# Two heads' attention scores computed together, a maximum moved from DVE to ACT, and fourteen low weight parts made by adding transfers

## The chip, the core and the metric

The kernel runs on one core of one Trainium2 chip. The metric is the device time of one execution in microseconds, smaller being better. Three runs of the kernel before gave 821.81, 825.79 and 827.91 us, so its median is 825.79 us. The core has five engines that work side by side and wait for each other by semaphores: TensorE (PE in the profile, its weight loads apart as PEld), VectorE (DVE), ScalarE (ACT), GpSimd (POOL) and SyncE (SP, which here only issues transfers). Each engine runs its own instructions in a fixed order, so an instruction that waits holds up everything behind it on that engine.

## The reference

One layer with three residual parts: a token mixer (stick-breaking attention with 8 heads of 64, a Conformer convolution branch and a state-space branch), a cross-attention into 256 memory tokens, and a SwiGLU feed-forward part. The sequence is 512 tokens of 1024 channels, all in float32. The change touches the stick-breaking attention and the loads of some weights:

```python
z = jnp.einsum('bhqd,bhkd->bhqk', qb, kh).astype(jnp.float32) * scale
mask = key_pos[None, :] < q_pos[:, None]
log_1mb = jnp.where(mask, jax.nn.log_sigmoid(-z), 0.0)
later = lax.cumsum(log_1mb, axis=3, reverse=True) - log_1mb
w = jnp.where(mask, jnp.exp(jax.nn.log_sigmoid(z) + later), 0.0)
return jnp.einsum('bhqk,bhkd->bhqd', w.astype(vh.dtype), vh)
```

The kernel uses that log_sigmoid(z) + later equals z minus the sum of softplus(z) over this key and all later ones, with softplus(z) = max(z, 0) + ln(1 + exp(-|z|)). So one weight is exp(z - running sum of softplus), the running sum going from the last key backwards.

## The kernel before

All matrix products are made of three products in a reduced float format (`mm3`, lines 114 to 116): each operand is split into a high part (a cast on ACT) and a low part (what is left), and high times high, low times high and high times low are added up in PSUM. Weights come through `load_w` (line 89): SP issues the load of a 128x1024 piece, ACT casts the high part (line 96), and the low part is made in one of two ways. Without `queue`, DVE subtracts the high part from the loaded piece (line 101). With `queue`, ACT writes the negated high part (line 98) and POOL issues a second transfer from memory that adds the weight to it (line 99). `load_k` (line 104) raises the priority of such a load by `EV_QUEUE`, so that it is started earlier. There are three buffers for loaded pieces and four each for high and low parts.

A scheduler orders the instructions of each engine from the program's order, priorities and its own estimates; parts in `tc.manual_schedule` keep the written order on the engines named.

The stage that the change touches is the attention chain `sb_chain` (line 774). It goes over four pairs of heads, and over six groups in each pair (`GROUPS`, line 707): one head with query block 3 (512 keys), block 2 (384 keys), or blocks 1 and 0 together (256 and 128 keys), the two heads of the pair in turn. `sb_weights` (line 709) makes the weights of a group: three products of 64 rows and a masking product into one of two PSUM banks with the tag `z` (lines 721 to 724), then on ACT the absolute value, exp and ln(1 + x) (lines 729 to 731), on DVE the maximum of z and zero added to it (line 732), the running sum (line 734), and z minus that (line 735), and exp on ACT again (line 736). For the groups with two blocks the running sum is one instruction over 384 columns, with a constant tile `seg` of ones and one zero that cuts it between the blocks; else a column of ones stands in its place. Two groups later (`DEPTH` is 2) `sb_turn` (line 743) transposes the weights on PE (line 748) and splits them (lines 120 and 121), and after the last group `sb_out` multiplies them with v.

After each group the chain yields a number (`SB_FILL`, the PE time in ns to be filled), and `weave` lets that much of other PE work in: the projections of the later pairs, the end of the convolution branch, the output projections `mixed_out` (line 804), the memory's norm, the keys of the cross-attention `kv("xa_wk", ...)` (line 862) and the output projection of the attention `out_sb` (line 813). In `mixed_out`, `out_sb` and `kv` the low parts of the weights are made on DVE; only the projections `sb_proj` (line 670), and two pieces in the feed-forward part, use the adding transfer.

Of the kernel before, what the change touches and what calls it, by code (L numbers as in the profile page):

```python
# [11 lines left out]
F32 = mybir.dt.float32  # L12
F32R = mybir.dt.float32r
AF = mybir.ActivationFunctionType
ALU = mybir.AluOpType
# [3 lines left out]
P = 128  # L19
SEQ = 512  # L20
D = 1024
KD = D // P
# [18 lines left out]
TQ, TK, TP = 4, 2, 2  # L41
# [31 lines left out]
def layer(ctx: ExitStack, tc: tile.TileContext, A: dict, out: bass.AP, dbg=None):  # L73
    nc = tc.nc
    v, s, g, te = nc.vector, nc.scalar, nc.gpsimd, nc.tensor
# [3 lines left out]
    const = ctx.enter_context(tc.tile_pool(name="const", bufs=1))  # L79
# [5 lines left out]
    def ps(tag, name):  # L85
        n = {"acc": 4, "z": 2, "tp": 2}[tag]
        return pp.tile([P, 512], F32, tag=tag, bufs=n, name=name)
# [16 lines left out]
    def load_k(w, k, n, name, queue=False):  # L104

        with tc.high_priority(offset=EV_QUEUE if queue else 0):
            return load_w(w[:, k:k + 2, :].rearrange("p k n -> p (k n)"), 2 * n, name, queue)
# [4 lines left out]
    def mm3(o, a, b, start, stop):  # L112

        te.matmul(o, a[0], b[0], start=start, stop=False)  # L114
        te.matmul(o, a[0], b[1], start=False, stop=False)  # L115
        te.matmul(o, a[1], b[0], start=False, stop=stop)  # L116
# [139 lines left out]
    ones1 = const.tile([P, 1], F32, name="ones1")  # L256
# [3 lines left out]
    pk = const.tile([P, NPK], F32, name="pk")  # L260
    negm = const.tile([P, P], F32R, name="negm")
    identr = const.tile([P, P], F32R, name="identr")
    seg = const.tile([P, 384], F32, name="seg")
    gqs = const.tile([P, 1], F32, name="gqs")
    rb = const.tile([P, 3, NT], F32, name="rb")

# [416 lines left out]
    def v_wait():  # L683

        return [x[:, 3, :].rearrange("p (t h d) -> p t h d", t=NT, h=2) for x in mxs]
# [20 lines left out]

    GROUPS = ((0, (3,)), (1, (3,)), (0, (2,)), (1, (2,)), (0, (1, 0)), (1, (1, 0)))

    def sb_weights(p, gi, qkT, sbp):

        qT, kT = qkT
        hh, qbs = GROUPS[gi]
        w = sum(qb + 1 for qb in qbs) * P
        r0 = slice(hh * 64, hh * 64 + 64)
        z = ps("z", f"z{p}{gi}")
        o = 0
        for qb in qbs:
            nk = (qb + 1) * P
            zo = z[:, o:o + nk]
            q, k = [x[r0, qb * P:(qb + 1) * P] for x in qT], [x[r0, 0:nk] for x in kT]  # L720
            te.matmul(zo, q[0], k[0], start=True, stop=False)  # L721
            te.matmul(zo, q[0], k[1], start=False, stop=False)
            te.matmul(zo, q[1], k[0], start=False, stop=False)
            te.matmul(zo[:, qb * P:], identr, negm, start=False, stop=True)  # L724
            o += nk
        ta = sbp.tile([P, SEQ], F32, tag="sba", bufs=2, name=f"sa{p}{gi}")[:, :w]
        ts = sbp.tile([P, SEQ], F32, tag="sbs", bufs=4, name=f"ss{p}{gi}")[:, :w]
        z = z[:, :w]
        s.activation(ta, z, AF.Abs)  # L729
        s.activation(ta, ta, AF.Exp, scale=-1.0)  # L730
        s.activation(ta, ta, AF.Ln, bias=1.0)  # L731
        v.scalar_tensor_tensor(ta, z, 0.0, ta, op0=ALU.max, op1=ALU.add)  # L732
        d0 = ones1.to_broadcast([P, w]) if len(qbs) == 1 else seg[:, ::-1]
        v.tensor_tensor_scan(ts[:, ::-1], d0, ta[:, ::-1], 0.0, op0=ALU.mult, op1=ALU.add)  # L734
        v.tensor_tensor(ts, z, ts, op=ALU.subtract)  # L735
        s.activation(ts, ts, AF.Exp)  # L736
        return ts
# [36 lines left out]
    def sb_chain(sbp):  # L774
        sqa = sbp.tile([P, SEQ], F32, name="sqa")
        wTs, pend = {}, []
        fronts = {0: sb_front(0, pr[0][0], sbp)}
        yield FRONT_FILL

        def turn():  # L780
            p, gi, ts = pend.pop(0)
            if gi == 0:
                wTs[p] = [[sbp.tile([P, 3, SEQ], F32R, tag=f"wT{i}{hh}", name=f"wT{i}{p}{hh}") for hh in range(2)] for i in "hl"]
            sb_turn(p, gi, ts, wTs[p])
            if gi == len(GROUPS) - 1:
                sb_out(p, wTs.pop(p), pr[p][1], sbp, sqa)

        for p in range(NPAIR):
            for gi in range(len(GROUPS)):
                pend.append((p, gi, sb_weights(p, gi, fronts[p], sbp)))  # L790
                if len(pend) > DEPTH:
                    turn()
                yield SB_FILL[p * 6 + gi]
                if gi == FRONT and p + 1 < NPAIR:
                    fronts[p + 1] = sb_front(p + 1, pr[p + 1][0], sbp)
                    if p + 1 == 3:
                        for x, y in zip(pr[3][1], v_wait()):
                            g.tensor_copy(x[:, :, ::2, :], y)
        while pend:
            turn()  # L800
        branch_rstd([sqa], 512, 0, sbp)


    def mixed_out(src, bi, ks, k0, hf):
        c = slice(hf * 512, hf * 512 + 512)
        acc = [ps("acc", f"wo{hf}{bi}{t}") for t in range(NT)]
        yield from gemm_rows(acc, lambda k, t: [x[:, k - k0, t * P:(t + 1) * P] for x in src], A["w_out"][hf], 512, ks,
                             f"wo{hf}{bi}", ks[0], ks[-1])
        for t in range(NT):
            with tc.high_priority(offset=EV_OUT):  # L810
                v.scalar_tensor_tensor(xr[:, t, c], acc[t], rb[:, bi, t:t + 1], xr[:, t, c], op0=ALU.mult, op1=ALU.add)  # L811

    def out_sb(ks):

        if ks[0] == 0:
            xacc.extend(ps("acc", f"wos{t}") for t in range(NT))
        for k in ks:
            if k % 2 == 0:
                wos[k // 2] = load_k(A["w_out"][0], k, 512, f"wos{k}")
            for t in range(NT):  # L820
                mm3(xacc[t], [x[:, k, t * P:(t + 1) * P] for x in mxs], cols(wos[k // 2], slice((k % 2) * 512, (k % 2) * 512 + 512)), k == 0, k == 3)
            tick()
            yield 2600

    xacc, wos = [], {}
# [36 lines left out]
    def kv(nm, hf):  # L862
        acc = [ps("acc", f"{nm}{hf}{t}") for t in range(2)]
        hm = mem["hm"]
        yield from gemm_rows(acc, lambda k, t: [hm[:, i, k, t * P:(t + 1) * P] for i in range(2)], A[nm][hf], 512, range(KD),
                             f"{nm}{hf}", 0, KD - 1, TK)
        for t in range(2):
            if nm == "xa_wv":
                c = slice(hf * 512, hf * 512 + 512)
                split(*[x[:, t, c] for x in mem["v"]], acc[t])  # L870
                continue
            kn = cvp.tile([P, 2, 256], F32, tag=("cpr", "ac")[t], name=f"kn{hf}{t}")
            ss = cvp.tile([P, 2], F32, tag="kss", bufs=2, name=f"kss{hf}{t}")
            av = acc[t].rearrange("p (h d) -> p h d", h=2)
            for h in range(2):
                s.activation(kn[:, h, :], av[:, h, :], AF.Square, accum_out=ss[:, h:h + 1])
            r = rstd(ss, 256, cvp, 2, "kr")
            for h in range(2):
                v.scalar_tensor_tensor(kn[:, h, :], av[:, h, :], r[:, h:h + 1], mem["g"], op0=ALU.mult, op1=ALU.mult)
            late.append([3 + t, lambda t=t, kn=kn: k_turn(hf, t, kn)])  # L880
# [10 lines left out]
    with tc.tile_pool(name="ssmp", bufs=1, side="right") as sp:  # L891
# [80 lines left out]
        with tc.manual_schedule(engines={v.engine, s.engine, g.engine}):  # L972
            for b in range(3):
                for x in vzs[b]:
                    g.memset(x[:, :, 1, :].bitcast(F32), 0.0)
            aside(18)
            squares(0)
            aside(2)
            scale(0)
            squares(1)  # L980
            turn(0)
            aside(2)
            u_high(0)
            scale(1)
            low(0)
            turn(1)
            squares(2)
            aside(99)
            g.memset(hp[:, :, :CPAD], 0.0)
            g.memset(tmpm, -2.0 ** 100)  # L990
            g.affine_select(out=tmpm, in_=tmpm, pattern=[[1, P]], compare_op=ALU.is_ge, fill=0.0, base=0, channel_multiplier=-1)
            g.memset(seg, 1.0)
            g.memset(seg[:, 255:256], 0.0)
            u_low(0)
            low(1)
            u_high(1)
            squares(3)
            scale(2)
            turn(2)
            u_low(1)  # L1000
            scale(3)
            turn(3)
            low(2)
            low(3)
            next(S5)
# [34 lines left out]
    kT = mem["k"]  # L1040
    with tc.tile_pool(name="xa", bufs=1, side="right") as xa:
# [29 lines left out]
        with tc.tile_pool(name="xq", bufs=1, side="right") as xq:  # L1071
            PT = [xq.tile([P, 2, 2, SEQ], F32R, name="PT" + i) for i in "hl"]
            qT = [xq.tile([P, 4, SEQ], F32R, name="qT" + i) for i in "hl"]
# [94 lines left out]
    with tc.tile_pool(name="ff", bufs=1, side="right") as ff:  # L1168
# [239 lines left out]
        for _, t, hf in slots:  # L1408
            for k in range(TAIL):
                step(NF - TAIL + k, *ops[k], t, hf)  # L1410
            c = slice(hf * 512, hf * 512 + 512)
# [59 lines left out]
```

## Time and profile before

| | |
|---|---|
| median of three runs | 825.79 us |
| profiled execution | 827.81 us, of which the span between its first and last instruction is 826.1 us |
| ACT busy over the span | 408.8 us (49%) |
| POOL busy over the span | 181.9 us (22%) |
| chain of work that ended last | PE 80%, DVE 12%, ACT 3% of the span |
| attention scores, first and last product (line 721) | 141.5 us and 283.8 us |

A profile gives for each engine the time that it was busy. A busy PE is not PE at its peak: its matrix products overlap, and its clock can be granted at half. The granted clock stands beside each stretch, 1.00 being full. The waits view says for which instruction an engine stood idle. In the lines of a group, the number behind x is how many there were, then come the busy time in us, the mean of one in ns, and the idle time before them.

### The profile page before, as it was taken

The page shows a single profiled execution, that of the slowest core. Times are in us where ns is not written, and L with a number is a line of the kernel's source. Part 1 is how long each engine was busy: PE and PEld are TensorE (multiplying, and loading weights), DVE is VectorE, ACT ScalarE, POOL GpSimd, SP SyncE. Part 2 cuts the span into 40 slices and gives each one's busy share as a digit, 9 for nine tenths or more (in the row PEclk, how much of TensorE's full clock was granted, in tenths as well). Part 3 has the DMA queues.
Part 4 walks back from the last instruction along what each step waited for, and adds up shares of the span by engine and source line. Part 5 has one row for each costly group of instructions (what it writes and reads, how often), then busy time and mean ns, then how long its engine had stood idle before and what let it go on. Part 6 is the DMA issues. An engine that isn't in the chain of part 4 may idle for free.

```text
span 826.1 us, 12223 instructions
## 1 busy us (share of the span) xinstructions
PE 786.6 (95%) x4640; PEld 689.5 (83%) x4640; DVE 632.4 (77%) x1095; ACT 408.8 (49%) x747; POOL 181.9 (22%) x157
## 2 busy tenths in 40 slices
PE   5699999999989999999999789999999999999998
PEld 3678999887767878888888689999999999888886
DVE  8979989789897968566856688899899998333333
ACT  6344375987667836354634653444444443323321
POOL 4910021001000000000000006577666671000000
PEclk9979999999888999999999979999999999999999
DMA  6233588543013423420442323333333321222322
GB/s 219 71 84 61 112 171 166 116 144 117 33 45 109 119 87 100 130 77 27 125 138 69 77 77 102 104 102 102 104 103 107 127 100 57 97 98 81 102 77 102
DMA packets 25115, 83.41 MB, mean 101 GB/s; under 512 B 3041, under 2 KB 3297, under 8 KB 25058
## 3 DMA queue, kind: packets, MB, share of 16 engines
q1 hardware_dynamic: 22466, 75.31, 28.7%
q0 software_dynamic: 2592, 7.34, 5.9%
q8 instruction: 36, 0.59, 0.3%
q14 instruction: 21, 0.17, 0.1%
HBM read 80.54 MB, written 2.10 MB: 100 GB/s over the span
## 4 chain that ended last, share of the span: by engine, by line
PE 80%; DVE 12%; ACT 3%; issue 2%; DMA 1%; POOL 0%; POOLq 0%; DVEq 0%
PE fo L114 5%; PE fo L116 5%; PE fo L115 5%; PE f L116 2%; PE f L115 2%; PE f L114 2%; PE xo L114 2%; PE xo L115 2%; PE qkv L114 2%; PE xo L116 2%; PE qkv L116 2%; PE qkv L115 2%; PE xq L114 2%; PE xq L115 2%; PE xq L116 2%
## 5 line engine op out<-in xcount | busy, mean ns | idle before, releaser
L618 DVE SCALAR_TENSOR_TENSOR cac<-hp,pk,cac 128x512 f32<-128x512 f32 x60 | 42.4, 748 | 0.0
L1251 POOL TENSOR_TENSOR wgb<-wgb 128x512 f32<-128x512 f32 x18 | 31.8, 1769 | 40.2 <-DMA wgb<-in_w_gu_dram 33.2
L1276 POOL TENSOR_TENSOR wga<-wga 128x512 f32<-128x512 f32 x20 | 28.8, 1439 | 43.5 <-DVE wga L1275 43.5
L1271 POOL DMA_DIRECT2D wa00lo<-in_w_gu_dram x1 | 0.9, 877 | 159.9 <-ACT wa00lo L1270 159.9
L1324 POOL TENSOR_TENSOR aF<-aF,fup 128x1024 f32<-128x1024 f32 x10 | 34.2, 3424 | 6.0 <-DVE fup L1320 5.1
L1252 POOL TENSOR_TENSOR wgb<-wga,wgb 128x512 f32<-128x512 f32 x18 | 35.4, 1965 | 0.3
L772 POOL TENSOR_TENSOR sqa<-sqa,sq 128x512 f32<-128x512 f32 x3 | 4.0, 1332 | 92.7 <-ACT sq L771 59.3
L1275 DVE TENSOR_TENSOR wga<-wgb,wga 128x512 f32<-128x512 f32 x22 | 22.9, 1039 | 0.0
L121 DVE TENSOR_TENSOR wTl<-wT,wTh 128x384 fp32r<-128x384 f32 (+2 forms) x40 | 16.3, 415 | 2.1 <-ACT wTh L120 2.0
L729 ACT ACTIVATE sa<-z 128x384 f32<-128x384 f32 (+1 forms) x24 | 12.6, 524 | 10.3 <-PE z L724 10.0
L120 ACT CAST wTh<-wT 128x384 fp32r<-128x384 f32 (+2 forms) x40 | 14.5, 369 | 6.2 <-PE wT L748 4.9
L734 DVE TENSOR_TENSOR_SCAN ss<-ones,sa 128x512 f32<-128x512 f32 (+1 forms) x16 | 17.3, 1082 | 0.0
L721 PE MATMUL z<-kh,qh 64*128 64x512 f32 (+3 forms) x32 | 13.6, 426 | 3.2 <-DVE ss L735 3.1
L736 ACT ACTIVATE ss<-ss 128x384 f32<-128x384 f32 (+1 forms) x24 | 13.5, 561 | 6.0 <-DVE ss L735 5.5
L732 DVE SCALAR_TENSOR_TENSOR sa<-z,sa 128x384 f32<-128x384 f32 (+1 forms) x24 | 14.2, 594 | 2.8 <-ACT sa L731 2.8
L721 PEld LDWEIGHTS z<-kh,qh 64*128 64x128 f32 x32 | 6.2, 192 | 10.8 <-DVE ss L735 5.2
L811 DVE SCALAR_TENSOR_TENSOR xr<-wo,rb,xr 128x512 f32<-128x512 f32 x16 | 11.9, 744 | 3.5 <-PE wo L116 3.2
L735 DVE TENSOR_TENSOR ss<-z,ss 128x384 f32<-128x384 f32 (+1 forms) x24 | 14.2, 592 | 0.0
L730 ACT ACTIVATE sa<-sa 128x384 f32<-128x384 f32 (+1 forms) x24 | 13.6, 565 | 0.3
L731 ACT ACTIVATE sa<-sa 128x384 f32<-128x384 f32 (+1 forms) x24 | 13.5, 564 | 0.3
L1322 ACT ACTIVATE aF<-aF 128x1024 f32<-128x1024 f32 x11 | 11.6, 1057 | 4.0 <-DVE aF L1320 2.9
L748 PE MATMUL wT<-ident,ss 128*128 128x128 f32 x80 | 12.6, 276 | 0.0
(2210 smaller groups left out, 3276.3 us busy)
## 6 DMA issues: line engine op xcount, KB each, us to landing
wgb<-in_w_gu_dram SPq DMA_DIRECT2D x22, 512.0 KB, 3.2
wga<-in_w_gu_dram SPq DMA_DIRECT2D x22, 512.0 KB, 3.4
for<-in_w_fo_dram SPq DMA_DIRECT2D x22, 512.0 KB, 3.3
xr<-in_x_dram SPq DMA_DIRECT2D x4, 512.0 KB, 5.1
out_dram<-xr SPq DMA_DIRECT2D x8, 256.0 KB, 2.0
xbh<-in_x_dram SPq DMA_DIRECT2D x2, 512.0 KB, 4.7
xbl<-in_x_dram SPq DMA_DIRECT2D x2, 512.0 KB, 7.6
mt<-in_mem_dram SPq DMA_DIRECT2D x2, 512.0 KB, 4.0
```

Source lines behind the costliest of these rows:

```text
L114: te.matmul(o, a[0], b[0], start=start, stop=False)
L115: te.matmul(o, a[0], b[1], start=False, stop=False)
L116: te.matmul(o, a[1], b[0], start=False, stop=stop)
L121: v.tensor_tensor(lo, src, hi, op=ALU.subtract)
L618: v.scalar_tensor_tensor(a, x, w, a, op0=ALU.mult, op1=ALU.add)
L721: te.matmul(zo, q[0], k[0], start=True, stop=False)
L734: v.tensor_tensor_scan(ts[:, ::-1], d0, ta[:, ::-1], 0.0, op0=ALU.mult, op1=ALU.add)
L1251: eng.tensor_tensor(b[:, 0], b[:, 1], b[:, 2], op=ALU.add)
L1252: eng.tensor_tensor(b[:, 1], a[:, 0], b[:, 1], op=ALU.subtract)
L1275: v.tensor_tensor(a[:, 0], b[:, 0], a[:, 0], op=ALU.subtract)
L1276: eng.tensor_tensor(a[:, 1], a[:, 1], a[:, 0], op=ALU.subtract)
L1324: (g if i + 1 < len(units) else v).tensor_tensor(aF[p], aF[p], dst, op=ALU.mult)
```

## The change

The products of the scores leave `sb_weights` and become `sb_scores`, which writes those of both heads of a pair, alternating, into both `z` banks before either head's further steps. On ACT, `sb_weights` gets one more instruction, the maximum of z and zero (Relu) into the tile of the running sum; the DVE instruction that did this is gone. The running sum takes two tensors, adding both; it is one instruction for each query block, and `seg` with its two memsets on POOL is gone. The loads in `mixed_out`, `out_sb` and `kv` for `xa_wk` use the adding transfer: 4 + 2 + 8 = 14 loads.

```diff
-    def sb_weights(p, gi, qkT, sbp):
+    def sb_scores(p, gi, qkT):
         qT, kT = qkT
-        hh, qbs = GROUPS[gi]
+        qbs = GROUPS[gi][1]
+        zs = [ps("z", f"z{p}{gi + hh}") for hh in range(2)]
+        with tc.manual_schedule(engines={te.engine}):
+            o = 0
+            for qb in qbs:
+                nk = (qb + 1) * P
+                for n, (i, j) in enumerate(((0, 0), (0, 1), (1, 0))):
+                    for hh, z in enumerate(zs):
+                        r0 = slice(hh * 64, hh * 64 + 64)
+                        te.matmul(z[:, o:o + nk], qT[i][r0, qb * P:(qb + 1) * P], kT[j][r0, 0:nk], start=n == 0, stop=False)
+                for z in zs:
+                    te.matmul(z[:, o + qb * P:o + nk], identr, negm, start=False, stop=True)
+                o += nk
+        return zs
+
+    def sb_weights(p, gi, z, sbp):
...
         s.activation(ta, z, AF.Abs)
+        s.activation(ts, z, AF.Relu)
         s.activation(ta, ta, AF.Exp, scale=-1.0)
         s.activation(ta, ta, AF.Ln, bias=1.0)
-        v.scalar_tensor_tensor(ta, z, 0.0, ta, op0=ALU.max, op1=ALU.add)
-        d0 = ones1.to_broadcast([P, w]) if len(qbs) == 1 else seg[:, ::-1]
-        v.tensor_tensor_scan(ts[:, ::-1], d0, ta[:, ::-1], 0.0, op0=ALU.mult, op1=ALU.add)
+        o = 0
+        for qb in qbs:
+            c = slice(o, o + (qb + 1) * P)
+            v.tensor_tensor_scan(ts[:, c][:, ::-1], ta[:, c][:, ::-1], ts[:, c][:, ::-1], 0.0, op0=ALU.add, op1=ALU.add)
+            o += (qb + 1) * P
         v.tensor_tensor(ts, z, ts, op=ALU.subtract)
         s.activation(ts, ts, AF.Exp)
         return ts
...
             for gi in range(len(GROUPS)):
-                pend.append((p, gi, sb_weights(p, gi, fronts[p], sbp)))
+                if gi % 2 == 0:
+                    zs = sb_scores(p, gi, fronts[p])
+                pend.append((p, gi, sb_weights(p, gi, zs[gi % 2], sbp)))
...
         yield from gemm_rows(acc, lambda k, t: [x[:, k - k0, t * P:(t + 1) * P] for x in src], A["w_out"][hf], 512, ks,
-                             f"wo{hf}{bi}", ks[0], ks[-1])
+                             f"wo{hf}{bi}", ks[0], ks[-1], queue=True)
...
-                wos[k // 2] = load_k(A["w_out"][0], k, 512, f"wos{k}")
+                wos[k // 2] = load_k(A["w_out"][0], k, 512, f"wos{k}", True)
...
         yield from gemm_rows(acc, lambda k, t: [hm[:, i, k, t * P:(t + 1) * P] for i in range(2)], A[nm][hf], 512, range(KD),
-                             f"{nm}{hf}", 0, KD - 1, TK)
+                             f"{nm}{hf}", 0, KD - 1, TK, queue=nm == "xa_wk")
```

## What was predicted

> **What bounds the kernel now.** I read the page first, then the busy times of stretches around the attention stage, then what PE waited for there, then the groups of instructions by line and shape, last the order in time.
>
> ```profile
> span 826.1 us, 12223 instructions
> PE 786.6 (95%) x4640; PEld 689.5 (83%) x4640; DVE 632.4 (77%) x1095; ACT 408.8 (49%) x747; POOL 181.9 (22%) x157
> ```
>
> Over the whole span PE is the busy engine. The change works between about 141 us, where the first score product starts, and 289 us, where the last weights of the chain are made. In that stretch the shares differ (columns: stretch and its length, then busy us and instructions of each engine, granted clock of PE, share of the DMA engines, GB/s):
>
> ```profile
> 141.00:289.00 148.00, 141.55 (x692) 111.89 (x691) 129.39 (x252) 112.53 (x256) 6.71 (x6) 0.93 0.35 98
> 207.20:214.00 6.80, 6.80 (x24) 5.42 (x22) 4.54 (x14) 4.28 (x11) 0.00 (x0) 0.51 0.22 81
> 231.10:234.50 3.40, 3.40 (x13) 2.95 (x13) 3.40 (x7) 3.11 (x6) 0.00 (x0) 0.52 0.00 0
> 244.80:255.00 10.20, 9.87 (x29) 7.69 (x30) 6.91 (x14) 4.63 (x8) 0.00 (x0) 0.51 0.44 125
> 260.00:280.00 20.00, 19.80 (x106) 15.10 (x105) 19.79 (x42) 18.19 (x47) 1.44 (x1) 1.00 0.31 93
> PE z L721 <- DVE ss L735: 3.1, 2, 1.7
> PE xa_wk L115 <- DVE xa_wk02l L101: 2.2, 1, 2.2
> ```
>
> DVE is busy 129.4 of 148 us, ACT 112.5. PE stood idle 3.1 + 2.2 = 5.3 us for DVE, in three waits. Beside each lies a stretch at half clock, 6.8 + 3.4 + 10.2 = 20.4 us in all. What half clock costs is seen in the order in time: equal products of 512 columns start 0.23 us apart at full clock and 0.42 us apart there.
>
> ```profile
> 223.97 0.39 PE L114 MATMUL wo<-wo110h,mxch 128*128 128x512 f32 x1
> 224.20 0.39 PE L115 MATMUL wo<-wo110l,mxch 128*128 128x512 f32 x1
> 250.54 0.63 PE L116 MATMUL xa_wk<-xa_wk02h,hm 128*128 128x512 f32 x1
> 250.96 0.63 PE L114 MATMUL xa_wk<-xa_wk02h,hm 128*128 128x512 f32 x1
> ```
>
> So about half of 20.4 us, 10.2 us, is lost to the clock. With the waits PE loses 15.5 us of this stage, all of it around moments when DVE is late: PE's own work would fit into 148 - 15.5 = 132.5 us. DVE is what is late in this stage, and the question is who is late next.
>
> **The change part by part.** These rows give the prices (line, engine, operation, shape, count, busy us, mean ns of one, idle us before):
>
> ```profile
> L732 DVE SCALAR_TENSOR_TENSOR sa<-z,sa 128x384 f32<-128x384 f32 x16 | 8.8, 549 | 1.4 <-ACT sa L731 1.4
> L732 DVE SCALAR_TENSOR_TENSOR sa<-z,sa 128x512 f32<-128x512 f32 x8 | 5.5, 683 | 1.4 <-ACT sa L731 1.4
> L734 DVE TENSOR_TENSOR_SCAN ss<-ones,sa 128x512 f32<-128x512 f32 x8 | 9.7, 1216 | 0.0
> L734 DVE TENSOR_TENSOR_SCAN ss<-seg,sa 128x384 f32<-128x384 f32 x8 | 7.6, 950 | 0.1
> L734 DVE TENSOR_TENSOR_SCAN ss<-ones,sa 128x384 f32<-128x384 f32 x8 | 7.6, 947 | 0.0
> L735 DVE TENSOR_TENSOR ss<-z,ss 128x384 f32<-128x384 f32 x16 | 8.8, 548 | 0.0
> L735 DVE TENSOR_TENSOR ss<-z,ss 128x512 f32<-128x512 f32 x8 | 5.5, 682 | 0.0
> L101 DVE TENSOR_TENSOR wo010l<-wo010s,wo010h 128x1024 fp32r<-128x1024 f32 x1 | 1.2, 1215 | 0.0
> L729 ACT ACTIVATE sa<-z 128x384 f32<-128x384 f32 x16 | 7.8, 490 | 6.4 <-PE z L724 6.1
> L729 ACT ACTIVATE sa<-z 128x512 f32<-128x512 f32 x8 | 4.8, 594 | 3.9 <-PE z L724 3.9
> L730 ACT ACTIVATE sa<-sa 128x384 f32<-128x384 f32 x16 | 8.4, 524 | 0.3
> L730 ACT ACTIVATE sa<-sa 128x512 f32<-128x512 f32 x8 | 5.2, 648 | 0.0
> L96 ACT CAST wo010h<-wo010s 128x1024 fp32r<-128x1024 f32 x1 | 1.1, 1060 | 0.0
> L96 ACT CAST ws34h<-ws34s 128x768 fp32r<-128x768 f32 x1 | 0.8, 841 | 0.0
> L98 ACT ACTIVATE ws34l<-ws34h 128x768 fp32r<-128x768 f32 x1 | 0.8, 848 | 0.0
> L99 POOL DMA_DIRECT2D ws36l<-in_w_sb_dram x1: 862/862/862, 159.6 to 159.6; - x1
> DMA to landing us min/median/max: 5.1/5.6/6.5
> ```
>
> *The maximum on DVE goes:* 8.8 + 5.5 = 14.3 us less on DVE. *Fourteen subtractions go:* 14 x 1.215 = 17.0 us less. *The running sum:* a second tensor in place of the ones costs nothing to see, since with the tile `seg` it took 950 ns and with ones 947 ns at 384 columns. The eight groups with two blocks are cut in two: from 512 to 384 columns the price falls by (1216 - 947) / 128 = 2.10 ns a column, so 256 columns take 678 ns and 128 take 409 ns, together 1087 instead of 950 ns: 8 x 0.14 = 1.1 us more. DVE then needs 129.4 - 14.3 - 17.0 + 1.1 = 99.2 us: it is no longer the bound.
>
> *The Relu on ACT* reads the same bank in the same shape as line 729: 7.8 + 4.8 = 12.6 us more. *Fourteen negated copies on ACT:* at 768 columns such a copy takes what the cast takes (848 and 841 ns), so at 1024 columns I take the cast's 1060 ns: 14 x 1.06 = 14.8 us more. ACT then needs 112.5 + 12.6 + 14.8 = 139.9 us by durations. Neighbours that do not wait for each other overlap on ACT by about 0.1 us: the next one starts 0.43 us after a start that took 0.52, and 0.73 after one that took 0.83.
>
> ```profile
> 158.04 0.52 ACT L736 ACTIVATE ss<-ss 128x384 f32<-128x384 f32 x1
> 158.47 0.83 ACT L98 ACTIVATE ws36l<-ws36h 128x768 fp32r<-128x768 f32 x1
> 159.20 0.63 ACT L635 COPY cn<-cl 128x256 f32<-128x256 f32 x2
> ```
>
> For 38 new instructions that is 3.8 us less, so ACT needs 136.1 to 139.9 us. It was the idler of the two and becomes the bound.
>
> *Fourteen more adding transfers:* POOL issues each in 0.86 us, 12 us on an engine that is busy 6.7 of 148 us; the DMA engines are 35% taken. A low part is there 1.06 + 0.86 + 5.6 x 1024 / 768 = 9.4 us after the high part instead of 1.2. I cost this at nothing, because the loads are raised in priority and the sixteen of this kind before left no wait of PE for a transfer; the cover is the distance of up to four buffers, and if it is gone each load costs up to 8.2 us. On POOL's queue they stand among the three additions of line 772, which come once in a pair of heads. The two memsets of `seg` at the start cost nothing either way.
>
> *The scores together on PE.* Eight heads x 3 products x 1280 columns are 60 widths of 512, at 0.23 us 13.8 us. One head's block shows a price for going from full-height to 64-row products and back: the second product starts 0.34 us after the first and the masking one 0.32 us after the third, where 0.23 would do, so some 0.2 us a block.
>
> ```profile
> 225.29 0.50 PE L721 MATMUL z<-kh,qh 64*128 64x512 f32 x1
> 225.63 0.39 PE L722 MATMUL z<-kl,qh 64*128 64x512 f32 x1
> 225.87 0.39 PE L723 MATMUL z<-kh,ql 64*128 64x512 f32 x1
> 226.19 0.33 PE L724 MATMUL z<-negm,identr 128*128 128x128 f32 x1
> 226.35 0.52 PE L177 MATMUL nmp<-ident,mt 128*128 128x128 f32 x3
> ```
>
> Two heads together halve the blocks from 32 to 16: 3.2 us less. If the two halves of the array also worked side by side, 6.9 us more would go; if each change of halves cost 0.1 us, 96 x 0.1 = 9.6 us would come. No row shows two halves in turn without a gap, so PE's work lies between 132.5 - 10.1 = 122.4 and 132.5 + 6.4 = 138.9 us. I take nothing for it: in the middle of that PE stays below ACT.
>
> **The sum.** The stage is set by ACT: 136.1 to 139.9 us of work, divided by how full its queue can be. ACT's fullest stretch above is 18.19 of 20 us, 0.91; that gives 149.6 to 153.8 us. DVE, as the late engine, reached 19.79 of 20, 0.99: 137.5 to 141.4 us. I take 0.96, nearer to DVE's, because what everything waits for has its inputs ready, but not all of it, because four ACT steps of a group hang on one another: 141.8 to 145.7, middle 143.7, so 148 - 143.7 = 4.3 us gained. The profiled execution took 827.81 us, its span 826.1; 827.81 - 4.3 = 823.5. The median of the three runs, 825.79, lies 2.0 us below it, so I predict **821.5 us**: within 1% of before, which is about what a measurement of this kernel can tell from no change.
>
> **The rivals.** *A, faster: ACT fills up as DVE did.* At 0.99 and the low end of its work the stage takes 137.5 us, 10.5 less: 815.3 us. For it speaks that DVE loses 30 us and with that all three of PE's waits and their half clock; against it that ACT's own idle time here is mostly before line 729, waiting for PE's scores (10.0 us), which more ACT work does not remove. Chance 0.35.
>
> Two rules of the Trainium skill bear on A. *TensorE: Matmul & The Clock Gate*, Part 1, says that the clock is halved after an idle window of about 3.4 us; the waits here were at most 2.2 us and half clock stood beside them all the same, so the trace does not bear the rule out as it stands. By it only the 5.3 us of waits would go with DVE's lateness, PE would need 142.7 us, and A would end near 820.5 us, not below. *TensorEngine Tiling (Array Packing)*, Key Properties, says that tiles of the array take products in parallel, and that a change of tiling mode drains it; the second agrees with the 0.2 us a block, the first no row here shows, and it would take the 6.9 us off PE again.
>
> *B, slower: the pair holds both banks.* Both `z` banks now come free together, after the second head's subtraction, and PE's next scores wait for that, with the side products queued behind them. The loop at 384 columns is: scores of two heads at most 2 x 1.06 = 2.1 us, eight ACT steps 2 x (2 x 0.490 + 2 x 0.524) = 4.1, running sum 0.95, subtraction 0.55: 7.7 us; at 512 columns 2.1 + 2 x (2 x 0.594 + 2 x 0.648) + 1.22 + 0.68 = 9.0; mean of three pairs of groups 8.1. Twelve are 97 us of 143.7, leaving 3.9 us each. ACT's eight steps take 4.4 us in the mean, twelve times 52 us; its other work is about 138 - 52 = 86 us, 7.1 us a pair. Once more than 3.9 of these 7.1 us, 55%, fall inside the loop, the loop decides; at 70% it takes 13.1 us, twelve 157 us, 9 us more than now: 835 us. Against it: before, two banks came free in turn and PE waited for them only twice. Chance 0.20.
>
> *C, the low parts land late:* if the four loads of `mixed_out`, with no load before them in their own product, each showed 8.2 us, 33 us would come: about 854 us. Against it the sixteen loads above. Chance 0.04.
>
> **How the numbers follow.** My forecast, 817.5 to 834 us, has 0.41; A 0.35; B and C 0.24. The forecast's own range goes from ACT at 0.99 with the long work (148 - 141.4 = 6.6 gained, 819) to ACT at 0.91 with it (5.8 lost, 831.6). To hold 8 in 10 the range reaches into A, to 809 (its 10.5 us, and some 6 more if a part of ACT's new work moves behind the stage, where the row below leaves ACT 11 us free), and to B's 835. Faster by over 1%, below 817.5: 0.35; within 1%: 0.41; slower by over 1%, above 834.0: 0.24.
>
> ```profile
> 289.00:306.00 17.00, 15.56 (x81) 12.48 (x79) 8.95 (x28) 5.81 (x14) 1.27 (x1) 1.00 0.24 76
> ```
>
> **What would show it.** DVE near 99 us and ACT near 138 us in the stage would prove the accounts; ACT near 0.96 of it, the bound. PE waiting for ACT instead of DVE would be my forecast; PE's scores waiting for the subtraction of line 735 would be B; PE waiting for a low part whose transfer is under way would be C. Full clock throughout and fewer PE waits would be A. Score products of both heads starting under 0.15 us apart at 512 columns would show the two halves side by side. The forecast is wrong if ACT stays below 130 us, or if the stage ends early though ACT is not full.

## The result, and the profile after

| | before | changed |
|---|---|---|
| median, same chips | 826.85 us (4 runs) | 860.43 us (4 runs, 858.45 to 862.29) |
| ratio | 1 | 1.0429, 95% interval 1.0383 to 1.0475 |
| span of the profiled execution | 826.1 us | 857.1 us |
| attention stage, first score product to last weights | 141 to 289 us | 141 to 323 us |

The changed kernel is slower by 4.3%: 34 us. The forecast was 821.5 us, with a range from 809 to 835. In the runs below, ratios leave out single disturbed executions (961.58 us in e8, 4223.69 us in e18, two of the kernel before), and e18's trace, taken in such a one, is not used. The page of the profile after begins so:

```profile
span 857.1 us, 12282 instructions
PE 788.7 (92%) x4640; PEld 689.8 (80%) x4640; DVE 609.4 (71%) x1065; ACT 430.0 (50%) x785; POOL 192.2 (22%) x169
```

PE's busy time went from 786.6 to 788.7 us: it has no more to do, it stands still longer. Where, the busy times of stretches tell (columns as in the prediction: stretch and length, then PE, PEld, DVE, ACT and POOL, granted clock, share of the DMA engines, GB/s):

```profile
141.00:323.00 182.00, 147.99 (x724) 116.50 (x722) 110.87 (x236) 135.73 (x299) 18.35 (x20) 0.90 0.52 127
260.00:280.00 20.00, 16.38 (x78) 12.38 (x76) 9.88 (x21) 15.56 (x40) 3.81 (x3) 0.95 0.83 210
```

The attention stage takes 182 us where it took 148. In it PE idles 182 - 148.0 = 34 us, against 148 - 141.6 = 6.4 before. And no engine is full: PE is busy 148.0 of 182 us, ACT, which was to set the stage, 135.7, DVE 110.9. When no engine is full and all of them wait, the amount of work does not explain the time, and the order of the work is the next place to look. The waits of the stage (engine, line, whom it waited for, us in total, times, longest):

```profile
PE z L720 <- DVE ss L742: 9.8, 8, 2.5
...
DVE ss L740 <- ACT sa L736: 25.8, 10, 14.6
```

DVE's running sum (line 740) waits 25.8 us for ACT's logarithm (line 736), 14.6 us of it once. A long single wait is a place to open in the order of time. There (start, duration, engine, line, operation; in brackets the idle time before and its releaser):

```profile
246.78 1.06 ACT L96 CAST xa_wk10h<-xa_wk10s 128x1024 fp32r<-128x1024 f32 x1
...
247.72 0.61 ACT L734 ACTIVATE ss<-z 128x512 f32<-128x512 f32 x1
248.21 1.07 ACT L98 ACTIVATE xa_wk10l<-xa_wk10h 128x1024 fp32r<-128x1024 f32 x1
...
249.57 0.86 POOL L99 DMA_DIRECT2D xa_wk10l<-in_xa_wk_dram  x1 [23.34 <-ACT xa_wk10l L98]
...
255.40 1.04 ACT L98 ACTIVATE xa_wk16l<-xa_wk16h 128x1024 fp32r<-128x1024 f32 x1
256.35 0.61 ACT L735 ACTIVATE sa<-sa 128x512 f32<-128x512 f32 x1
...
257.60 0.50 PE L115 MATMUL xa_wk<-xa_wk10l,hm 128*128 128x512 f32 x1 [3.61 <-DMA xa_wk10l<-in_xa_wk_dram]
...
261.92 1.05 ACT L96 CAST wos0h<-wos0s 128x1024 fp32r<-128x1024 f32 x1 [4.96 <-PE xa_wk L116]
262.88 0.63 ACT L736 ACTIVATE sa<-sa 128x512 f32<-128x512 f32 x1
...
263.53 1.22 DVE L740 TENSOR_TENSOR_SCAN ss<-sa,ss 128x512 f32<-128x512 f32 x1 [14.58 <-ACT sa L736]
```

Read ACT's lines from top to bottom. The second head's Relu is at 247.72, its exponential (line 735) only at 256.35 and its logarithm (736) at 262.88. Eight casts and copies of weights stand between the Relu and the logarithm, and a ninth, `xa_wk10h`, just ahead of the Relu. The last, the cast `wos0h`, had to wait 4.96 us: it writes a buffer that products of `xa_wk10` were still reading, and those had waited 3.61 us for their low part, issued at 249.57 and landed at 257.6. ACT did not pass over the waiting cast, and the logarithm stood behind it. The Trainium skill (*PSUM — Partial Sum Buffer*, Engine vs sequencer instructions) says that ScalarE's queue is strictly first in, first out; the 4.96 us before the logarithm agree with it. I call this the second place.

The first place is earlier, where the second pair of heads reaches its third group. The order in time on PE, changed kernel:

```profile
200.28 0.53 PE L720 MATMUL z<-kh,qh 64*128 64x384 f32 x1
...
207.88 0.44 PE L720 MATMUL z<-kh,qh 64*128 64x384 f32 x1
208.24 0.50 PE L114 MATMUL o<-wTh,vzh 128*128 128x512 f32 x1
...
209.37 0.44 PE L720 MATMUL z<-kl,qh 64*128 64x384 f32 x1
...
212.57 0.28 PE L116 MATMUL o<-wTh,vzl 128*128 128x128 f32 x1
212.78 0.44 PE L720 MATMUL z<-kl,qh 64*128 64x384 f32 x1
212.78 0.61 PE L720 MATMUL z<-kh,ql 64*128 64x384 f32 x2
213.32 0.44 PE L722 MATMUL z<-negm,identr 128*128 128x128 f32 x2
```

The first head's first score product runs at 200.28, the second head's at 207.88, and the last ones end after 213.32. From 207.88 on, the 24 products of `o`, the output of the pair before, stand between them. ACT and DVE at the same place:

```profile
205.66 0.69 DVE L742 TENSOR_TENSOR ss<-z,ss 128x512 f32<-128x512 f32 x1
...
212.40 0.63 ACT L852 ACTIVATE msq<-mt 128x512 f32<-128x512 f32 x1 [3.75 <-DMA mt<-in_mem_dram]
...
215.34 0.67 ACT L123 ACTIVATE mxsh<-o,pk 128x512 fp32r<-128x512 f32 x1
215.91 0.47 ACT L733 ACTIVATE sa<-z 128x384 f32<-128x384 f32 x1
...
221.97 0.54 DVE L742 TENSOR_TENSOR ss<-z,ss 128x384 f32<-128x384 f32 x1
```

The scores were there by 213.8, but ACT takes the group's absolute value (line 733) only at 215.91. Ahead of it in ACT's order stand four squares of the memory's rows (line 852), the first of which waited 3.75 us for its transfer, and the split of `o` (`mxsh`). So PE's order is not all that holds this group up. Its subtraction comes at 222.0 us, 16.3 us after the one ahead of it. In the run e8 below the products stand together, and the subtraction comes at 206.5 us, 6.9 us after its predecessor. Of the 15.5 us between the two kernels 6.1 were lost earlier (205.7 against 199.6 us for the predecessor), and 9.4 fall inside the group.

### The profile page after: what moved, and what is told of

It is laid out like the page before. It is cut to its first block, busy times and chain, and to the rows that moved or that the text cites. A ratio compares the mean times of both kernels' runs of the same rounds, so it can differ in the third digit from the quotient of the medians.

```text
span 857.1 us, 12282 instructions
## 1 busy us (share of the span) xinstructions
PE 788.7 (92%) x4640; PEld 689.8 (80%) x4640; DVE 609.4 (71%) x1065; ACT 430.0 (50%) x785; POOL 192.2 (22%) x169
## 4 chain that ended last, share of the span: by engine, by line
PE 67%; DVE 14%; issue 7%; ACT 5%; DMA 4%; POOL 1%; SPq 0%; DVEq 0%; POOLq 0%; ACTq 0%
PE fo L115 5%; PE fo L116 5%; PE fo L114 5%; PE xo L114 2%; PE xo L115 2%; PE xo L116 2%; PE qkv L116 2%; PE qkv L114 2%; PE qkv L115 2%; PE xq L114 2%; PE xq L116 2%; PE xq L115 2%; PE f L116 2%; PE f L114 2%; PE f L115 2%
## 5 line engine op out<-in xcount | busy, mean ns | idle before, releaser
L740 DVE TENSOR_TENSOR_SCAN ss<-sa,ss 128x512 f32<-128x512 f32 (+3 forms) x32 | 26.6, 848 | 25.8 <-ACT sa L736 25.8
L121 DVE TENSOR_TENSOR wTl<-wT,wTh 128x384 fp32r<-128x384 f32 (+2 forms) x40 | 16.6, 417 | 11.2 <-ACT wTh L120 10.8
L755 PE MATMUL wT<-ident,ss 128*128 128x128 f32 x80 | 15.3, 314 | 5.1 <-ACT ss L743 4.7
L755 PEld LDWEIGHTS wT<-ident,ss 128*128 128x128 f32 x80 | 10.4, 159 | 7.3 <-ACT ss L743 5.8
L1329 ACT ACTIVATE aF<-aF 128x1024 f32<-128x1024 f32 x11 | 11.6, 1057 | 3.0 <-DVE aF L1327 2.9
```

Of the source, the lines that this page charges most:

```text
L740: v.tensor_tensor_scan(ts[:, c][:, ::-1], ta[:, c][:, ::-1], ts[:, c][:, ::-1], 0.0, op0=ALU.add, op1=ALU.add)
L755: te.transpose(pt[:, b * P:(b + 1) * P], ts[:, b * P:(b + 1) * P], ident)
```

## The experiments

The change has three parts: the pair scores, Relu with the two-tensor sum, and fourteen adding transfers. First each alone and in twos, then the transfers taken apart. All times are medians; ratios are to the kernel before on the same chips.

| run | what it is | us | ratio, 95% interval |
|---|---|---|---|
| e1 | before + 14 adding loads | 828.95 | 1.0050 [1.0020, 1.0079] |
| e2 | changed, without the 14 loads | 821.82 | 0.9953 [0.9928, 0.9978] |
| e3 | before + Relu and sum | 821.74 | 0.9958 [0.9929, 0.9986] |
| e4 | before + pair scores | 832.78 | 1.0085 [1.0049, 1.0121] |
| e5 | loads + Relu and sum | 840.59 | 1.0206 [1.0149, 1.0264] |
| e6 | loads + pair scores | 843.71 | 1.0238 [1.0175, 1.0302] |
| e7 | changed, no raise on the 14 loads | 851.47 | 1.0334 [1.0277, 1.0390] |
| e8 | changed, 8 key loads by DVE | 824.49 | 0.9989 [0.9956, 1.0022] |
| e9 | e8 + raise + ACT's copy | 842.53 | 1.0230 [1.0192, 1.0268] |
| e10 | changed, keys' copies on POOL | 839.13 | 1.0193 [1.0157, 1.0228] |
| e11 | e8 + raise + bytes | 840.90 | 1.0218 [1.0175, 1.0260] |
| e12 | e8 + raise, low part on POOL | 843.48 | 1.0242 [1.0200, 1.0284] |
| e13 | e8 + raise | 840.04 | 1.0190 [1.0117, 1.0263] |
| e14 | changed, plain key loads not raised | 856.19 | 1.0385 [1.0333, 1.0436] |
| e15 | changed, keys not raised | 834.61 | 1.0129 [1.0073, 1.0186] |
| e16 | e8, low part on POOL, no raise | 838.47 | 1.0171 [1.0121, 1.0222] |
| e17 | changed, chain raised too | 862.07 | 1.0480 [1.0400, 1.0559] |
| e18 | e8, chain raised | 844.77 | 1.0230 [1.0170, 1.0290] |

### One part, or all but one (e1 to e4)

e1 is the kernel before with the three `queue` edits of the diff; e2 the changed kernel without them, of which one is shown:

```diff
-                             f"{nm}{hf}", 0, KD - 1, TK, queue=nm == "xa_wk")
+                             f"{nm}{hf}", 0, KD - 1, TK)
```

> Theory L (the 14 adding transfers: their casts and negated copies, raised in priority, stand in ACT's queue ahead of the chain, and their low parts land late): most of the 34 us comes with this edit alone, 845 to 862 us. Theory P (the pair holds both banks of z): this edit alone changes little, 818 to 834 us. Theory F (ACT is too full): half way, 830 to 845 us, with ACT above 0.9 of the stage.

> The changed kernel with the low parts of the 14 loads made on DVE as before. Theory L: the loss is gone, 812 to 830 us. Theory P: most of it stays, 840 to 862 us. Theory F: 825 to 840 us, since ACT has 15 us less to do.

e3 adds Relu and the sum to the kernel before, and e4 the pair scores:

```diff
+        s.activation(ts, z, AF.Relu)
-        v.scalar_tensor_tensor(ta, z, 0.0, ta, op0=ALU.max, op1=ALU.add)
```

> The kernel before with only the maximum on ACT and the running sum of two tensors. All theories: within 8 us of before; theory F puts it above (up to 834 us), theories L and P at or below (815 to 828 us), since DVE loses 13 us and ACT gains 12.6.

> The kernel before with only the scores of two heads together. Theory P: the loss is here, 840 to 862 us, with PE's scores waiting for the subtraction of line 735. Theories L and F: 810 to 830 us, lower because the two halves of the array work side by side (some 7 us of PE).

Alone, the loads cost 0.5%, the pair 0.9%, and Relu with the sum gives 0.4%. That adds up to 0.9%, 8 us, of the 4.3%. Without the loads the rest is as fast as e3 (0.9953 and 0.9958): beside Relu the pair costs nothing that shows. So 4.8% appears when the loads meet the rest.

### Two parts, and two ways to weaken the loads (e5 to e8)

e5 and e6 join the loads with one other part each. e7 takes the raise in priority off the fourteen loads (`up` is set for the sixteen older ones alone), and e8 leaves the eight `xa_wk` loads to DVE, not raised, and keeps the other six:

```diff
-        with tc.high_priority(offset=EV_QUEUE if queue else 0):
+        with tc.high_priority(offset=EV_QUEUE if up else 0):
```

> Loads and Relu with its running sum, scores head by head. Both put work on ACT (27 us together). Theory F2 (the two loads of ACT together are the loss): 845 to 862 us. Theory P2 (the loss needs the pair, which frees both banks late, together with casts in ACT's queue): 820 to 832 us, about the sum of the two edits alone.

> Loads and scores of two heads together, the maximum on DVE. Theory P2: most of the loss, 845 to 862 us. Theory F2: the sum of the two edits alone, 832 to 842 us.

> The changed kernel, the 14 loads without the raised priority. If the raised casts, which wait in ACT's queue for a buffer with the chain behind them, are the cause (the 15 us hole at 248 to 263 us and the like): 820 to 838 us. If the bytes of the adding transfers are the cause (the loads of xr and mt came late): 848 to 862 us.

> The changed kernel, the eight loads of xa_wk back on DVE; mixed_out and out_sb keep their six adding transfers. If the hole at 248 to 263 us, where four xa_wk casts stand in front of the chain, is its own loss: 835 to 848 us (15 us or more back). If the late xr at 177 to 190 us decides: 848 to 860 us.

The loads with Relu cost 2.1%, with the pair 2.4%, each between what its two theories gave: no one partner is needed. e8 takes back the whole loss, so it hangs on the eight loads of the keys' weights. In e7 PE does wait for low parts under way:

```profile
PE xa_wk L115 <- DMA xa_wk16l<-in_xa_wk_dram: 5.1, 1, 5.1
PE xa_wk L115 <- DMA xa_wk12l<-in_xa_wk_dram: 4.1, 1, 4.1
PE wo L115 <- DMA wo120l<-in_w_out_dram: 3.7, 1, 3.7
```

With seven shorter ones such waits are 23.1 us. In the changed kernel, with the raise, two are left in the stage, 4.2 us.

### What in these eight loads costs (e9 to e12)

e9, e11 and e12 start from e8 and put one thing back; e10 starts from the changed kernel and moves ACT's copies. The raise came with all of them. `queue == 2` marks the keys' loads; the four branches stand in the order e9, e10 (the adding transfer follows it), e11 (DVE's subtraction follows it), e12:

```diff
+        if queue == 2:
+            s.activation(lo[:, :n], hi[:, :n], AF.Copy, scale=-1.0)
+            v.tensor_tensor(lo[:, :n], st[:, :n], hi[:, :n], op=ALU.subtract)
...
+            g.tensor_scalar(lo[:, :n], hi[:, :n], -1.0, None, op0=ALU.mult)
...
+            g.dma_start(spare[name], src)
...
+            g.tensor_tensor(lo[:, :n], st[:, :n], hi[:, :n], op=ALU.subtract)
```

> The changed kernel with the keys' eight low parts again by DVE's subtraction (824.5 us in the eighth run), and of the taken-out path only ACT's negated copy put back, with the raise: the copy is written and then overwritten by DVE, no transfer is added. Theory 'lateness' (the low part lands 8 to 12 us after the cast, holds the four buffers that long, and the casts that wait for a buffer stand in ACT's queue ahead of the chain): 824 to 830 us. Theory 'ACT's time' (8.5 us of copies in ACT's queue ahead of the chain are enough): 845 us or more. Theory 'bytes' (4 MB more slow the other loads): 824 to 826 us.

> The changed kernel with all its adding transfers, the keys' eight negated copies written by POOL, not by ACT. Theory 'lateness': the low part lands later still, some 2 to 3 us by POOL's 128x512 rows of 1.4 to 1.8 us, so 858 to 870 us. Theory 'ACT's time': 825 to 835 us. Theory 'bytes': as the changed kernel, about 860 us.

> As the first of this set, but of the taken-out path only the eight transfers are put back, from the weights to a spare place in memory that nothing reads; no negated copy, the low part by DVE, the raise kept. Theory 'bytes': 845 us or more. Theory 'lateness' and theory 'ACT's time': 824 to 830 us.

> The changed kernel with the keys' eight low parts subtracted on POOL: no copy on ACT, no transfer, nothing on DVE, raise kept. By POOL's 128x512 rows (1.4 to 1.8 us) a 128x1024 subtraction takes some 3 us, so the low part is ready some 3.5 us after the cast, where the transfer took 8 to 12 us. Theory 'lateness': 820 to 830 us, and lower than the run with DVE's subtraction only if DVE's 11 us count; the other two theories expect the same, so this one tells whether a third way keeps what the other parts give.

None of the three theories of these expectations (lateness, ACT's time, bytes) held. Copy, bytes and a low part on POOL cost the same, 2.2 to 2.4%, and so does the full transfer once ACT is rid of its copies (e10, 1.9%). What the four share is the raise.

### The raise alone, and the transfers without it (e13 to e16)

e13 is e8 with nothing but the raise on the eight loads. e14 is the changed kernel with the raise only from the cast on, so that the plain loads keep their place on SP. e15 is the changed kernel without the raise on the keys. e16 makes the low parts on POOL, without the raise.

```diff
-        with tc.high_priority(offset=EV_QUEUE if queue else 0):
+        with tc.high_priority(offset=EV_QUEUE if queue and "xa" not in name else 0):
```

> The changed kernel with the keys' eight low parts by DVE's subtraction, as in the 824.5 us run, and nothing but the raise in priority put back on these eight loads. Theory 'order' (the raise moves SP's plain loads of these weights between and ahead of the rows of x and of the memory, and the casts ahead of the chain in ACT's queue): 838 to 844 us, with the subtraction of the third group of the second pair near 218 us (206.5 without the raise). Rival 'each part costs by itself' (a copy, the bytes, POOL each some 17 us): 823 to 827 us.

> The changed kernel; only the plain loads of the keys' weights keep their old priority, the casts, copies and adding transfers stay raised. SP's order is then that of the 824.5 us kernel, but for one load. Theory 'order through SP': the first 15 us go, the subtraction of the third group of the second pair near 207 us, the whole 842 to 848 us, for the copies and the landing still cost the second 17 us. If the casts in ACT's queue carry the first part too: 855 to 862 us.

> The changed kernel, the keys' eight loads not raised, the other six still raised, all fourteen by adding transfers. Theory 'order': the first part goes, but TensorE now waits for the low parts, 3 to 5 us each for some of them: 840 to 850 us. Rival 'the raise is all of it': 824 to 828 us.

> The changed kernel, the keys' eight low parts subtracted on POOL and nothing of them raised. Theory 'order': within 3 us of the 824.5 us run with DVE's subtraction, 821 to 828 us. Rival 'each part costs by itself': 840 to 845 us as with POOL and the raise.

e13 settles the first question: the raise alone costs 2.0% with DVE doing the subtraction. e9, e11 and e12 lie inside its interval, so beside the raise the copy, the bytes and POOL's subtraction show no cost of their own. The other three fell outside what the order theory gave: e14 took longer than 842 to 848 us, e15 less than 840 to 850, and e16 longer than 821 to 828. e8, e13, e15 and the changed kernel make a table of two by two (ratios):

| low parts of the keys | not raised | raised | the raise costs |
|---|---|---|---|
| by DVE | 0.9989 (e8) | 1.0190 (e13) | 2.0% |
| by adding transfers | 1.0129 (e15) | 1.0429 (changed) | 3.0% |
| the transfers cost | 1.4% | 2.4% | both: 4.4% |

The four ratios are known to 0.3 to 0.7% either way, so 2.0 and 3.0%, or 1.4 and 2.4%, are hardly told apart.

The stage in e8, e15 and e13 shows the same, by PE's idle time: 147 - 135.9 = 11.1 us, 156 - 136.1 = 19.9 us, and in e13 18.2 us by 289 us, where its chain still had 14 us to go:

```profile
141.00:288.00 147.00, 135.91 (x715) 106.33 (x713) 115.11 (x242) 126.59 (x291) 10.68 (x12) 0.97 0.45 123
```

```profile
141.00:297.00 156.00, 136.06 (x706) 106.08 (x704) 104.25 (x226) 132.70 (x296) 17.52 (x20) 0.95 0.59 143
```

```profile
141.00:289.00 148.00, 129.80 (x670) 102.32 (x669) 109.03 (x227) 117.00 (x265) 9.37 (x11) 0.95 0.47 121
```

What the raise does can be read from the order in which each engine's instructions ran. SP's (e8's lines with -, e13's with +, start times left out):

```
-DMA xr<-in_x_dram 128x1024 x4
+DMA xr<-in_x_dram 128x1024
 DMA xa_wk02s<-in_xa_wk_dram 128x1024
+DMA xr<-in_x_dram 128x1024 x3
```

A plain load of a raised weight now stands between rows of `x`. The raise covers the plain load too, which the prediction did not count. But e14, with SP's order put back but for one load, still stands at 1.0385: SP is not the main way. On PE and ACT the order changes as well, and there the two places divide the kernels so:

| kernel | `o` products between the second head's score and masking products | subtraction of that group, us | casts and copies between Abs and logarithm, second place | subtraction there, us after the one before |
|---|---|---|---|---|
| e8 | 0 | 206.5 | 0 | 2.3 |
| e15 | 0 | 208.3 | 0 | 2.2 |
| e7 | 0 | 209.9 | 0 | 2.3 |
| e16 | 21 | 217.5 | 0 | 2.2 |
| e11 | 24 | 218.1 | 1 | 3.2 |
| e13 | 24 | 218.7 | 1 | 3.2 |
| e10 | 24 | 219.1 | 1 | 3.2 |
| e9 | 21 | 221.5 | 0 | 2.2 |
| e12 | 24 | 221.6 | 1 | 4.5 |
| e14 | 24 | 217.6 | 9 | 16.6 |
| changed | 24 | 222.0 | 9 | 16.6 |

All eight kernels with the output's products inside the group have its subtraction 7.6 to 15.5 us later than the three without. They share a second thing: on ACT three or four squares of the memory's rows and the split of `o` stand ahead of the group's absolute value, where in e8, e15 and e7 it comes ahead of the squares. In seven of the eight the first square waits 1.7 to 4.8 us for its transfer. Which of the two orders costs how much was not tested apart. The two kernels with nine casts and copies ahead of the logarithm lose some 14 us there, the others 2.3 us at most. e16 has the first place without a raise: the raise is one way to it, and not the only one. And e7 has neither place and still takes 851 us; PE's 23.1 us of waits for low parts are what its trace shows in their stead. For comparison the products in e8, within 1 us but for the first head's first one at 193.62:

```profile
201.12 0.44 PE L720 MATMUL z<-kh,qh 64*128 64x384 f32 x1
201.12 0.61 PE L720 MATMUL z<-kl,qh 64*128 64x384 f32 x2
201.40 0.50 PE L720 MATMUL z<-kh,ql 64*128 64x384 f32 x2
201.83 0.44 PE L722 MATMUL z<-negm,identr 128*128 128x128 f32 x2
```

### Putting the chain ahead again (e17, e18)

If the loads cost time because they overtook the chain, raising the chain by the same amount should undo it:

```diff
+                with tc.high_priority(offset=EV_QUEUE):
                     if gi % 2 == 0:
                         zs = sb_scores(p, gi, fronts[p])
                     pend.append((p, gi, sb_weights(p, gi, zs[gi % 2], sbp)))
```

> The changed kernel, all of it, and the chain's scores and weights raised in priority by the same amount as the fourteen loads. In the order that results the products of the third group of the second pair stand together ahead of the output's, and the chain's exponentials and logarithms of the third pair ahead of the keys' casts. Theory 'order' (the loads went ahead of the chain in queues kept in order): the two holes of 15 and 17 us go, 822 to 832 us. Rival 'the loads' work and landing times themselves': 850 to 862 us.

> The 824.5 us kernel (the changed kernel with the keys' low parts by DVE, those loads not raised), and the chain raised in the same way. Theory 'order': its order had no such place, so 818 to 828 us; below 820 us if the chain was still held up in smaller ways. Rival: the chain ahead leaves TensorE's side work to run out earlier, 830 us or more.

Both missed: 862 us, no faster than the change itself, and from e8 the chain's raise alone costs 2.4%. In e17 both places are gone, as meant: the group of the first place is through at 191.7 us and not at 222.0. But the subtraction of the second head beside it comes only at 227.5, no earlier than in the changed kernel (227.5). ACT's order in e17 shows why:

```profile
216.28 1.05 ACT L96 CAST xa_wk04h<-xa_wk04s 128x1024 fp32r<-128x1024 f32 x1
222.44 0.63 ACT L853 ACTIVATE msq<-mt 128x512 f32<-128x512 f32 x1 [5.12 <-DMA mt<-in_mem_dram]
...
225.38 0.47 ACT L734 ACTIVATE ss<-z 128x384 f32<-128x384 f32 x1
```

Its Relu (line 734) stands behind the keys' casts and behind a square that waits 5.12 us for rows of the memory. PE's next scores wait 6.75 us for that subtraction. So the hole came back in another place. The step from "these two places" to "put them right and the time comes back" is not shown: the places were put right, a third stood there, and no time came back.

## Why the prediction was wrong, point by point

**The step that failed** is "I cost this at nothing, because the loads are raised in priority and the sixteen of this kind before left no wait of PE for a transfer". The raise was counted as cover and not as a cost. On the keys' eight loads it costs 2.0 to 3.0% (e8 to e13, e15 to the changed kernel), and the transfers themselves 1.4 to 2.4%. The moved instructions were priced in ACT's and POOL's time, 14.8 and 12 us, and not in their place in the queue: casts, copies and plain loads were put ahead of a chain that hangs together step by step. That the order is how the raise costs its time is read from the traces; e17 and e18 did not prove it. The sixteen older loads were also a narrow sample: in the kernel before, the two adding transfers of the feed-forward part left PE waits of 2.9 and 2.7 us:

```profile
PE f L116 <- DMA wa01lo<-in_w_gu_dram: 2.9, 1, 2.9
PE f L116 <- DMA wa00lo<-in_w_gu_dram: 2.7, 1, 2.7
```

**"The stage is set by ACT" at 0.96** fell with it. ACT had 135.7 us of work, 136.1 to 139.9 were forecast, but in 182 us: 0.75 full. DVE had 110.9 us where 99.2 were forecast. Both stand in a stretch 34 us longer than the one they were forecast for, so they are no clean test of the accounts, but neither engine set the time. e2, where the loads are away, shows what the other two parts do: 0.9953, some 4 us gained.

**The prices.** Relu and the copies on ACT came as forecast: 7.9 + 4.8 = 12.7 us against 12.6, and 1.06 us a copy. The cut sum was priced at 678 and 409 ns, and measured at 684 and 402:

```profile
L734 ACT ACTIVATE ss<-z 128x384 f32<-128x384 f32 x16 | 7.9, 495 | 0.0
L734 ACT ACTIVATE ss<-z 128x512 f32<-128x512 f32 x8 | 4.8, 606 | 0.0
L98 ACT ACTIVATE wo010l<-wo010h 128x1024 fp32r<-128x1024 f32 x1 | 1.1, 1063 | 0.0
L740 DVE TENSOR_TENSOR_SCAN ss<-sa,ss 128x256 f32<-128x256 f32 x8 | 5.5, 684 | 4.6 <-ACT sa L736 4.6
L740 DVE TENSOR_TENSOR_SCAN ss<-sa,ss 128x128 f32<-128x128 f32 x8 | 3.2, 402 | 0.0
```

**The pair scores at nothing.** Beside Relu that holds (e3 against e2). Without it (e4) the pair costs 0.9%, 7 us, just past the slow end of the 10.1 gained to 6.4 lost that the prediction allowed.

**The landing** was put at 7.5 us by size alone. In the changed kernel the low parts of 512 KB took 7.1 to 11.6 us, the longest of them under way until 268 us, in part of the stretch where the DMA engines were 0.83 busy:

```profile
wo020l<-in_w_out_dram POOLq DMA_DIRECT2D x1, 512.0 KB, 7.1
...
wo010l<-in_w_out_dram POOLq DMA_DIRECT2D x1, 512.0 KB, 11.0
...
xa_wk16l<-in_xa_wk_dram POOLq DMA_DIRECT2D x1, 512.0 KB, 11.6
```

**The rivals.** C, the low parts late, had the mechanism of e7 and a part of the second place (3.61 us of PE, then 4.96 of ACT), and its 854 us lay nearest; it was given 0.04 because the sixteen loads before left no wait. B, the pair holding both banks, shows in PE's waits for the subtraction, 9.8 us in eight against 3.1 in two before, and does not decide: e2 has the pair and is faster than before. A, the faster, needed a full ACT. What none of the cases held was a loss by order with no engine full; that is why the range ended at 835.

**What stays open.** Why the loads cost 0.5% alone and 2.1 to 2.4% beside either other part: e5 and e6 lose time in other places than the changed kernel, and those were not taken apart. And whether any order of the changed kernel brings it below 822 us; e17 and e18 tried one. No version beat e2 and e3, which are 0.4% to 0.5% below before.

## What to carry to other kernels

A raise in priority is a move, and its price has to be sought in what then stands behind the moved work in each queue that it touches, casts and plain loads too; adding up busy times did not show it here. Where no engine would be full after a change, compare the compiled order around the chain before trusting a sum, and look for waiting work ahead of the chain and for side work inside its groups. And a part that costs 0.5% alone is not proved cheap: test it together with the parts that it will meet.

## What the runs showed of the hardware

Score products of the two heads, in the two halves of the array, start within 0.01 us of each other, where equal products of 512 columns one after another started 0.23 us apart, so the halves do work side by side:

```profile
243.03 0.50 PE L720 MATMUL z<-kh,qh 64*128 64x512 f32 x1
243.03 0.49 PE L720 MATMUL z<-kl,qh 64*128 64x512 f32 x1
243.36 0.39 PE L720 MATMUL z<-kh,ql 64*128 64x512 f32 x1
243.37 0.40 PE L720 MATMUL z<-kl,qh 64*128 64x512 f32 x1
```

No row of the kernel before could show that. The rule of the Trainium skill that tiles of the array take products in parallel (*TensorEngine Tiling (Array Packing)*, Key Properties) agrees with these rows. It bought no time that shows: e2, with the pair, and e3, without, take the same.
